# Branch products one pair later, w_out's splits over twelve stages, and one more step behind each softmax, in a hybrid decoder layer

## The chip, the cores and the metric

The kernel runs on one NeuronCore of a Trainium2 chip. The metric is device time in microseconds (us), from the start to the end of one execution. Five engines work beside each other, each through its own queue in order: TensorE (PE; its weight loads are listed apart as PEld), VectorE (DVE), ScalarE (ACT), GpSimd (POOL) and SyncE (SP), which only starts DMA transfers here. An instruction waits at the head of its queue until what it needs is there, and everything behind it waits too.

## The reference, cut to what matters

One layer of a decoder, for a prompt of 1024 tokens and for 64 sample tokens (8 × 8). `D` is 1024, `W` is 512.

```python
h = rmsnorm(x, g_pre)
proj = h @ w_in                         # 7 slices of W columns, then 3 merge gates of D columns
p_in, p_gate, c_val, c_glu, c_gate, q, x_gate = [proj[..., i * W:(i + 1) * W] for i in range(7)]
merge_logits = proj[..., 7 * W:].reshape(B, S, 3, D)
a = pool_mix(...) * silu(p_gate)                                      # branch 0
u = c_val * sigmoid(c_glu)
bconv = silu(layernorm(causal_dwconv(u, width 31))) * silu(c_gate)    # branch 1
p = softmax(qh @ mk / sqrt(128))                                      # 4 heads, 256 memory tokens
cattn = (p @ mv) * silu(x_gate)                                       # branch 2
br = einsum('bsnw,nwd->bsnd', stack([a, bconv, cattn]), w_branch)
merged = sum_n sigmoid(merge_logits)[n] * br[n]
y = merged @ w_out
x_new = x + rmsnorm(y, g_post)
```

## The kernel before

**Products.** Everything is held transposed: channels on the 128 partitions, the 1088 tokens along the row. Matrices are float32; each operand is split into a float16 part and the float16 rest (`hilo`: L75 on ACT for the first, L77 or, with a scale, L79 on DVE for the rest), and a product is three matmuls per piece of the inner dimension (`mm3`, L85, L88, L89). The projections and the output product use a Strassen-like scheme: `pair` (for a pair of 128-column blocks of w_in) makes seven products of twelve matmuls of 512 columns over seven sums of weights and the seven sums of h, which lie split in `BO` under the names `B11`, `T1`, `T2`, `B21`, `T3`, `T4`, `B22`. The sums of weights are made by accumulating DMAs on POOL's queue (L499 to L507), a `post` (L466) on DVE finishes an output block, and the 64 sample tokens get small products of 64 columns. `sig_pair` is a pair for gates, with the sigmoid (L664) on ACT.

**Branches and merge.** `merge(bi, ...)` multiplies branch `bi` with its part of w_branch and with its gates and sums over the branches, for four pairs of output tiles (`dp`). Call the gates of a pair G0 to G3 (seven stages each) and its branch products B0 to B3 (six stages each: two tiles by three groups of 364, 364 and 360 tokens, `TOK`; the third holds the samples). A branch product is twelve matmuls of 364 columns into a bank `pb`; L1151 on DVE multiplies the bank with the gate tile. The gated tile becomes `M[d]` in the first merge; in later ones an accumulating DMA (L1157) on POOL's queue adds it, and for the last pair of the last merge a DVE add (L1153). Stages run G0 B0 G1 B1 G2 B2 G3 B3. The merges come as 2 (attention), 0 (pooling), 1 (convolution).

**What sets the order.** The kernel writes a list `stages`. The main loop emits, at stage s: the loads of stage s + 12, the weight sums of s + 8, the weight splits of s + 3, the matmuls of s, a number of convolution taps (`conv_step`: L714, one DVE instruction of 1024 columns per tap, 31 taps for each of four channel tiles), the evictions of s, what hangs behind s, and some steps of the *jobs*. Taps and job steps per stage are the section's rates. A job is a generator (the heads' attention `head`, the samples' attention, the pooling groups, the convolution's samples); each `yield` ends a step. `until("prompt", bi)` behind a stage runs jobs until that branch's prompt part is there. A scheduler then places the emitted instructions on the engines' queues.

**Attention.** `head` does scores, `softmax_rows` (maximum L823, exponential L826, reciprocal L828, scaling L830), and in the next step the transposes (L851 on PE) and the product with the values. `sample_attention` does the same for the samples (transposes L935); at its end L951 multiplies the attention's output with its gate and L75/L77 split it into X[2], the operand of merge(2)'s third token group. `conv_samples` and the start of the convolution (L712, L725, L728, L729) share DVE and POOL with it.

**Buffers.** `Q` is a ring of 20 large buffers (gate tiles, M, X, keys, taps, w_out's first four row blocks), `raw` one of 4 for weights, `ws` one of 13 for split weights; PSUM has 4 banks `pm` and 4 banks `pb`.

**The tail.** Behind merge(1) comes `out_pair`, the product with w_out. It uses the places in `BO`, which become free as the last gates end: `wo_split` splits pieces of w_out into a freed place (L75, L79), `wo_less` subtracts blocks of w_out on POOL (L1208). A table hangs them on the stages from `last_pair`, the first stage of G3 in merge(1). `samples_split` (L77, 128x64) splits the samples' part of M.

## Time and profile before

| | |
|---|---|
| times of three runs | 934.6, 937.97, 1017.92 us (median 937.97) |
| profiled execution | 935.87 us, span 933.8 us |
| mean granted TensorE clock | 0.970 |
| instructions | 15219 |
| HBM read, written | 62.37 MB, 6.33 MB |

The span is what the profile's records cover, the execution's own time is 2.1 us longer. Times of the stages are counted from the span's start. In the profile, `pm L85 <- ...` names the tile written, the line of the instruction, and behind the arrow what was waited for; numbers behind tile names are left out.

```profile
## 2 busy tenths in 40 slices
PE   5869999899999869999989989999999999968996
...
DVE  4698599999968999999999696559565544699876
...
PEclk8889999999999988999999999999999999998998
```

Each digit is the busy share, in tenths, of one of 40 equal slices of 23.3 us; the last row is the granted clock of TensorE. Slices 1 to 3 are the start-up, the tenth to fourteenth the heads' and samples' attention, the fifteenth to twenty-first merge(2) and the pooling projections beside the taps, the last four the end of merge(1) and the output product.

### The profile page before, as it was taken

To read this page: it belongs to the slowest core of one execution; us is meant where nothing else is said; L and a number is where in the kernel's file an instruction comes from. 1 tells how busy PE (TensorE), PEld (TensorE's weight loads), DVE (VectorE), ACT (ScalarE), POOL (GpSimd) and SP (SyncE) were. 2 spreads that over 40 slices of the span, in tenths; PEclk is the share of its full clock that TensorE was granted. 3 is DMA by queue.
4 is the path that set the end of the run, shared out by engine and by line. 5 is a ranking of instruction groups with operands and counts; after the bars stand their busy time and mean duration, and the time that the engine had idled before them with its cause. 6 is when DMAs were issued, how large, how long until landed. Compare 5 with 4: busy or idle time off the path is not lost.

```text
span 933.8 us, 15219 instructions
## 1 busy us (share of the span) xinstructions
PE 858.4 (92%) x5765; PEld 459.7 (49%) x5765; DVE 741.3 (79%) x1141; ACT 452.8 (48%) x964; POOL 359.3 (38%) x384
## 2 busy tenths in 40 slices
PE   5869999899999869999989989999999999968996
PEld 3325444554455435555444545555545555535532
DVE  4698599999968999999999696559565544699876
ACT  7767446564653613323345444346445443545542
POOL 1364152344243380311235664516364213285500
PEclk8889999999999988999999999999999999998998
DMA  8635742225556222334444345545554656310132
GB/s 296 160 62 157 205 107 57 58 68 136 126 191 159 91 39 79 70 79 93 97 97 102 73 102 116 121 97 105 123 122 101 138 131 216 85 57 24 69 124 90
DMA packets 99238, 103.23 MB, mean 111 GB/s; under 512 B 5231, under 2 KB 71781, under 8 KB 99149
## 3 DMA queue, kind: packets, MB, share of 16 engines
q1 hardware_dynamic: 82748, 68.24, 23.3%
q0 software_dynamic: 16416, 34.02, 20.4%
q8 instruction: 45, 0.74, 0.3%
q14 instruction: 29, 0.23, 0.1%
HBM read 62.37 MB, written 6.33 MB: 74 GB/s over the span
## 4 chain that ended last, share of the span: by engine, by line
PE 40%; DVE 20%; issue 3%; DMA 2%; ACT 1%; POOL 0%; DVEq 0%; ACTq 0%; POOLq 0%
PE pm L85 10%; PE pm L88 9%; PE pm L89 9%; DVE q L714 6%; PE pb L88 4%; PE pb L89 3%; PE pb L85 3%; DVE ws L79 3%; DVE ws L77 2%; DMA raw<-raw 2%; DVE BO L79 1%; DVE q L1151 1%; DVE q L466 1%; DVE q L1090 1%; DVE q L1082 1%
## 5 line engine op out<-in xcount | busy, mean ns | idle before, releaser
L85 PE MATMUL pm<-BO,ws 128*128 128x512 f16 x836 | 320.7, 385 | 18.6 <-DVE q L787 4.8
L88 PE MATMUL pm<-BO,ws 128*128 128x512 f16 x836 | 321.2, 384 | 2.2 <-DVE BO L79 1.6
L89 PE MATMUL pm<-BO,ws 128*128 128x512 f16 x836 | 320.3, 384 | 1.2 <-DVE ws L77 0.9
L79 DVE SCALAR_TENSOR_TENSOR ws<-raw,ws 128x512 f16<-128x512 f32 x228 | 194.2, 869 | 60.1 <-ACT ws L75 58.5
L88 PEld LDWEIGHTS <-ws 128*128 128x128 f16 x1548 | 149.1, 99 | 135.4 <-issue 29.9
L85 PEld LDWEIGHTS <-ws 128*128 128x128 f16 x1548 | 148.8, 99 | 126.1 <-issue 17.2
L89 PEld LDWEIGHTS <-ws 128*128 128x128 f16 x1548 | 149.2, 99 | 123.5 <-issue 8.2
L75 ACT ACTIVATE ws<-raw 128x512 f16<-128x512 f32 x228 | 138.1, 625 | 121.8 <-PE pm L89 50.4
L714 DVE SCALAR_TENSOR_TENSOR q<-q,cw,q 128x1024 f32<-128x1024 f32 x120 | 174.2, 1462 | 0.2
L85 PE MATMUL pb<-q,ws 128*128 128x364 f16 (+1 forms) x288 | 92.2, 323 | 13.2 <-ACT q L75 8.4
L88 PE MATMUL pb<-q,ws 128*128 128x364 f16 (+1 forms) x288 | 92.5, 321 | 0.0
L89 PE MATMUL pb<-q,ws 128*128 128x364 f16 (+1 forms) x288 | 92.3, 321 | 0.0
L499 POOL DMA_DIRECT2D raw<-raw x25 | 21.9, 876 | 157.6 <-ACT raw L498 133.3
L513 ACT ACTIVATE h<-pm 128x512 f32<-128x512 f32 x75 | 44.2, 590 | 63.5 <-PE pm L89 63.3
L1151 DVE SCALAR_TENSOR_TENSOR q<-pb,q 128x364 f32<-128x364 f32 (+1 forms) x72 | 37.2, 527 | 22.1 <-PE pb L89 20.4
L466 DVE SCALAR_TENSOR_TENSOR q<-pm,h 128x512 f32<-128x512 f32 x51 | 34.8, 683 | 23.1 <-PE pm L89 13.2
L75 ACT ACTIVATE q<-q 128x1024 f16<-128x1024 f32 (+2 forms) x37 | 35.7, 972 | 29.6 <-DVE q L863 15.5
L507 POOL DMA_DIRECT2D raw<-raw x25 | 23.4, 935 | 66.3 <-issue 16.8
L506 POOL DMA_DIRECT2D raw<-raw x25 | 21.7, 867 | 65.6 <-DMA raw<-raw 25.3
L77 POOL TENSOR_TENSOR q<-q,q 128x1024 f16<-128x1024 f32 (+1 forms) x17 | 32.5, 1921 | 30.2 <-ACT q L75 30.2
L498 ACT ACTIVATE raw<-raw 128x512 f32<-128x512 f32 x50 | 30.9, 625 | 26.4 <-DVE ws L79 26.2
L85 PE MATMUL pm<-BS,ws 128*128 128x64 f16 x416 | 43.7, 194 | 0.0
(242 smaller groups left out, 1311.9 us busy)
## 6 DMA issues: line engine op xcount, KB each, us to landing
raw<-in_w_in SPq DMA_DIRECT2D x104, 256.0 KB, 3.0
raw<-raw POOLq DMA_DIRECT2D x100, 256.0 KB, 3.2
q<-in_x_prompt SPq DMA_DIRECT2D x16, 512.0 KB, 9.4
q<-q POOLq DMA_DIRECT2D x14, 544.0 KB, 5.8
raw<-in_w_branch SPq DMA_DIRECT2D x24, 256.0 KB, 3.8
q<-in_w_mem_kv SPq DMA_DIRECT2D x8, 512.0 KB, 6.8
q<-in_cache_mem_k SPq DMA_DIRECT2D x8, 512.0 KB, 3.7
q<-in_cache_mem_v SPq DMA_DIRECT2D x8, 512.0 KB, 9.4
```

What stands on the lines that cost most here:

```text
L75: nc.scalar.activation(hi, src, AF.Copy, scale=scale)
L77: (eng or nc.vector).tensor_tensor(lo, src, hi, ALU.subtract)
L79: nc.vector.scalar_tensor_tensor(lo, src, scale, hi, ALU.mult, ALU.subtract)
L85: ins = nc.tensor.matmul(out, wh, xh, start=start and j == 0, stop=False, skip_group_check=partial)
L88: nc.tensor.matmul(out, wh, xl, start=False, stop=False, skip_group_check=partial)
L89: nc.tensor.matmul(out, wl, xh, start=False, stop=stop and j == n - 1, skip_group_check=partial)
L466: nc.vector.scalar_tensor_tensor(dst, ps, sc, base, ALU.mult, ALU.add)
L498: nc.scalar.activation(A(1, kh), A(1, kh), AF.Copy, scale=-1.0)
L507: nc.gpsimd.dma_start(out=A(0, 1), in_=A(0, 0), accum_op=ALU.add)
L513: nc.scalar.activation(v[name], ps, AF.Copy, scale=sc)
L714: ins = nc.vector.scalar_tensor_tensor(acc, src, wj, acc, ALU.mult, ALU.add)
L1151: nc.vector.scalar_tensor_tensor(g, p, 1.0 / WS, g, ALU.mult, ALU.mult)
```

## The change

In `merge` the gates of the next pair are emitted ahead of the branch products of a pair: G0 G1 B0 G2 B1 G3 B2 B3. What hung behind G0 (`until("prompt", bi)`) now hangs behind G1. `last_pair` moves with G3, from 13 to 19 stages before the end of the sections, and the table of w_out's splits goes from 10 to 14 stages behind it. In `head` and in `sample_attention` one more `yield` stands between the softmax and the transposes. Lines behind the edits move by 1, 2 or 11: L935 becomes L937, L951 L953, L1007 L1009, L1151 L1162, L1153 L1164, L1157 L1168, L1208 L1219.

```diff
--- before.py
+++ after.py
@@ -844,6 +844,7 @@
                     mm3(p[:, a, :], [(q[:, 0, tk : tk + P], q[:, 1, tk : tk + P], kT[:, 0, h, :], kT[:, 1, h, :])])
                 softmax_rows(p, 2, prs[:, tp * 2 : tp * 2 + 2, :])
             yield
+            yield
             pT = Q([P, 2, 2, HALF], F16)
             for c in range(2):
                 p = pb()
@@ -929,6 +930,7 @@
             vr = kr
             pr = half((P, 1, NMEM))
             softmax_rows(sc[:, :NMEM].rearrange("p (a m) -> p a m", a=1), 1, pr)
+            yield
             yield
             p = pb()
             for c in range(2):
@@ -1117,9 +1119,18 @@
     M = [None] * KT
 
     def merge(bi, first, last):
+
+        sgs = []
+
+        def gates(dp):
+            if dp < KT // 2:
+                sgs.append({})
+                sig_pair(GATE0 + bi * D + dp * 2 * P, sgs[dp])
+
+        gates(0)
         for dp in range(KT // 2):
-            sg = {}
-            sig_pair(GATE0 + bi * D + dp * 2 * P, sg)
+            gates(dp + 1)
+            sg = sgs[dp]
             if dp == 0:
                 after(until("prompt", bi))
             v = {}
@@ -1187,7 +1198,7 @@
         section()
 
 
-    last_pair = len(stages) - 13
+    last_pair = len(stages) - 19
     WO = [None] * KT
     gp = {}
 
@@ -1212,12 +1223,12 @@
     for s, f in [
         (0, lambda: (wo_split(B11, 0, 0), wo_less(0, 1, (0, 1), (0, 0)))),
         (2, lambda: wo_split(T1, 0, 1)),
-        (5, lambda: wo_split(B21, 1, 0)),
-        (6, lambda: (wo_split(B22, 1, 1), wo_less(1, 1, (1, 1), (0, 1)))),
-        (7, lambda: wo_split(T2, 1, 1)),
-        (8, lambda: wo_less(0, 0, (1, 1), (0, 0))),
-        (9, lambda: (wo_split(T3, 0, 0), wo_less(1, 0, (1, 0), (1, 1)))),
-        (10, lambda: wo_split(T4, 1, 0)),
+        (6, lambda: wo_split(B21, 1, 0)),
+        (8, lambda: (wo_split(B22, 1, 1), wo_less(1, 1, (1, 1), (0, 1)))),
+        (10, lambda: wo_split(T2, 1, 1)),
+        (11, lambda: wo_less(0, 0, (1, 1), (0, 0))),
+        (12, lambda: (wo_split(T3, 0, 0), wo_less(1, 0, (1, 0), (1, 1)))),
+        (14, lambda: wo_split(T4, 1, 0)),
     ]:
         stages[last_pair + s][4].append(f)
```

How this moves instructions is seen at three places. The first is TensorE's queue at the samples' softmax, first before the change: `h_3253` and `h_3360` are the softmax's result, `pb_3074` and `pb_3154` its scores, `pm` banks belong to gates, `pb` banks with 364 columns to branch products.

```order
L88 MATMUL pb_3074<-q_3205,q_1311 32x256
L89 LDWEIGHTS q_1311
L89 MATMUL pb_3074<-q_3205,q_1311 32x256
L935 MATMUL pb_3261<-ident,h_3253 128x128 x2
L85 LDWEIGHTS ws_3272
L85 MATMUL pb_3516<-q_1633,ws_3272 128x364
L88 LDWEIGHTS ws_3272
L88 MATMUL pb_3516<-q_1633,ws_3272 128x364
```

Behind the change the same place of the queue reads (`...` stands for gate matmuls):

```order
L88 LDWEIGHTS q_1311
L88 MATMUL pb_3154<-q_3333,q_1311 32x256
L89 LDWEIGHTS q_1311
L89 MATMUL pb_3154<-q_3333,q_1311 32x256
L85 LDWEIGHTS ws_3368
L85 MATMUL pm_3387<-BO,ws_3368 128x512
...
L89 LDWEIGHTS ws_3823
L89 MATMUL pm_3888<-BO,ws_3823 128x512
L937 MATMUL pb_3404<-ident,h_3360 128x128 x2
L742 MATMUL pb_3620<-ident,q_2722 30x128
L743 MATMUL pb_3620<-ident,v_3621 64x128
```

Before, the transposes (L935) follow the last score product. After, 27 gate matmuls stand between: twelve into `pm_3387`, twelve into `pm_3862` and three into `pm_3888`; the rows left out are these.

The second is VectorE's queue around L787 of `q_4902`, the last gate step of the pooling branch before which TensorE is held, first before the change. L714 are convolution taps, L794 the samples' piece of the same gates, L1007 (L1009) a pooling group's product, L79 splits of weights.

```order
L466 SCALAR_TENSOR_TENSOR h_4900<-pm_4824,h_4898 128x512
L79 SCALAR_TENSOR_TENSOR ws_5061<-raw_4631,ws_5061 128x512
L77 TENSOR_TENSOR q_4785<-q_4779,q_4785 128x1024
L794 SCALAR_TENSOR_TENSOR q_4883<-pm_4908,q_4883 128x64
L714 SCALAR_TENSOR_TENSOR q_3952<-q_2856,cw,q_3952 128x1024
L787 SCALAR_TENSOR_TENSOR q_4902<-pm_4800,q_4902 128x512
L79 SCALAR_TENSOR_TENSOR ws_5115<-raw_4634,ws_5115 128x512
L794 SCALAR_TENSOR_TENSOR q_4902<-pm_4908,q_4902 128x64
L466 SCALAR_TENSOR_TENSOR h_4999<-pm_4824,h_4863 128x512
L714 SCALAR_TENSOR_TENSOR q_3952<-q_2856,cw,q_3952 128x1024
L1007 SCALAR_TENSOR_TENSOR q_4883<-pb_5004,psc,q_4883 128x364
L79 SCALAR_TENSOR_TENSOR ws_5151<-raw_4848,ws_5151 128x512
```

Behind the change, around the same L787, the queue reads:

```order
L714 SCALAR_TENSOR_TENSOR q_3962<-q_2799,cw,q_3962 128x1024
L79 SCALAR_TENSOR_TENSOR ws_4978<-raw_4848,ws_4978 128x512
L79 SCALAR_TENSOR_TENSOR ws_4984<-raw_4631,ws_4984 128x512
L79 SCALAR_TENSOR_TENSOR ws_5025<-raw_4845,ws_5025 128x512
L794 SCALAR_TENSOR_TENSOR q_4883<-pm_4908,q_4883 128x64
L79 SCALAR_TENSOR_TENSOR ws_5028<-raw_4848,ws_5028 128x512
L466 SCALAR_TENSOR_TENSOR h_4900<-pm_4824,h_4898 128x512
L79 SCALAR_TENSOR_TENSOR ws_5061<-raw_4631,ws_5061 128x512
L794 SCALAR_TENSOR_TENSOR q_4902<-pm_4908,q_4902 128x64
L1009 SCALAR_TENSOR_TENSOR q_4883<-pb_5004,psc,q_4883 128x364
L787 SCALAR_TENSOR_TENSOR q_4902<-pm_4800,q_4902 128x512
L79 SCALAR_TENSOR_TENSOR ws_5115<-raw_4634,ws_5115 128x512
```

Before, taps alternate with the splits up to and past L787; after, the last tap (`q_3962`) stands ten rows ahead of it, and one L794 and one L1009 more stand ahead of it. In the whole queue ahead of L787 there are 117 taps before and 120 after; ahead of the earlier L466 of `q_4667` (529 rows in), 103 and 109.

The third is VectorE's queue at the split of w_out into `B22`, first before the change. `BO<-raw` and `BO<-q` are rests of w_out, `ws_8600` the samples' part of M, L1151 (L1162) branch products.

```order
L79 SCALAR_TENSOR_TENSOR BO<-raw_8128,BO 128x512
L79 SCALAR_TENSOR_TENSOR BO<-raw_8158,BO 128x512
L466 SCALAR_TENSOR_TENSOR q_8200<-pm_8145,h_8172 128x512
L79 SCALAR_TENSOR_TENSOR BO<-raw_8174,BO 128x512
L79 SCALAR_TENSOR_TENSOR BO<-raw_8203,BO 128x512
L77 TENSOR_TENSOR ws_8600<-q_3238,ws_8600 128x64
L77 TENSOR_TENSOR ws_8600<-q_3291,ws_8600 128x64
L77 TENSOR_TENSOR ws_8600<-q_3733,ws_8600 128x64
L77 TENSOR_TENSOR ws_8600<-q_3755,ws_8600 128x64
L77 TENSOR_TENSOR ws_8600<-q_4055,ws_8600 128x64
L77 TENSOR_TENSOR ws_8600<-q_4077,ws_8600 128x64
L1151 SCALAR_TENSOR_TENSOR q_8200<-pb_8349,q_8200 128x364
```

Behind the change the rows at the split of `B22` are:

```order
L1162 SCALAR_TENSOR_TENSOR q_7793<-pb_8222,q_7793 128x364
L79 SCALAR_TENSOR_TENSOR BO<-raw_8033,BO 128x512
L79 SCALAR_TENSOR_TENSOR BO<-raw_8066,BO 128x512
L466 SCALAR_TENSOR_TENSOR q_8108<-pm_8053,h_8080 128x512
L79 SCALAR_TENSOR_TENSOR BO<-raw_8082,BO 128x512
L1162 SCALAR_TENSOR_TENSOR q_7793<-pb_8236,q_7793 128x364
L79 SCALAR_TENSOR_TENSOR BO<-raw_8111,BO 128x512
L79 SCALAR_TENSOR_TENSOR BO<-raw_8033,BO 128x512
L1162 SCALAR_TENSOR_TENSOR q_7793<-pb_8262,q_7793 128x360
L79 SCALAR_TENSOR_TENSOR BO<-raw_8066,BO 128x512
L79 SCALAR_TENSOR_TENSOR BO<-q_7975,BO 128x512
L1162 SCALAR_TENSOR_TENSOR q_7813<-pb_8280,q_7813 128x364
```

Before, the samples' splits stand behind the splits of `B22` and ahead of the last branch evictions; after, the evictions of B2 and B3 alternate with the splits of w_out, and the eight samples' splits come twelve to twenty-two rows behind the last of them.

## Prediction

> **What bounds the kernel now.** I read the page first, then busy time by stage, then TensorE's waits, then the rows around each wait. The two page lines are busy us, share of the span and instruction count per engine, and the costliest VectorE group.
>
> ```profile
> PE 858.4 (92%) x5765; PEld 459.7 (49%) x5765; DVE 741.3 (79%) x1141; ACT 452.8 (48%) x964; POOL 359.3 (38%) x384
> L714 DVE SCALAR_TENSOR_TENSOR q<-q,cw,q 128x1024 f32<-128x1024 f32 x120 | 174.2, 1462 | 0.2
> ```
>
> TensorE at 92% is the bound on average, but an average says nothing of a stage. The next rows are windows: from:to in us, length, then busy time and count of PE, PEld, DVE, ACT and POOL, the granted clock, DMA share, GB/s.
>
> ```profile
> 98.00:334.00 236.00, 223.04 (x1611) 123.79 (x1610) 204.15 (x288) 125.71 (x262) 90.65 (x78) 0.99 0.44 115
> 316.00:322.00 6.00, 4.13 (x18) 2.42 (x19) 5.93 (x9) 3.75 (x6) 1.48 (x1) 0.72 0.29 103
> 334.00:502.00 168.00, 152.87 (x1027) 80.64 (x1026) 168.00 (x192) 60.04 (x120) 49.70 (x45) 0.96 0.37 80
> 345.00:355.00 10.00, 5.92 (x30) 2.77 (x30) 10.00 (x13) 2.73 (x8) 3.36 (x2) 0.50 0.11 20
> 450.00:460.00 10.00, 8.09 (x64) 3.96 (x62) 10.00 (x12) 3.42 (x8) 4.41 (x6) 0.83 0.30 54
> 486.00:496.00 10.00, 7.35 (x37) 3.36 (x35) 10.00 (x9) 3.43 (x7) 6.16 (x5) 1.00 0.49 128
> 560.00:820.00 260.00, 258.92 (x1740) 141.33 (x1739) 153.09 (x248) 122.62 (x245) 100.60 (x99) 1.00 0.53 122
> 829.00:854.00 25.00, 19.22 (x131) 9.90 (x131) 24.45 (x45) 10.22 (x32) 17.83 (x26) 0.80 0.24 74
> ```
>
> From 560 to 820 PE is busy 258.92 of 260 at full clock, so whatever moves inside those 260 us can't bring anything. From 334 to 502 VectorE is busy 168.00 of 168: there it is the bound, and PE waits for its queue. In 98 to 334 VectorE idles 236 − 204.15 = 31.85 us. So three places can give time: the attention stretch before 334, the VectorE stretch, and the tail from 820. Their waits, as waiter, what released it, total us, times, longest:
>
> ```profile
> PE pb L935 <- DVE h L830: 4.0, 1, 4.0
> PE pb L851 <- DVE q L830: 3.7, 5, 1.6
> PE pb L85 <- ACT q L75: 8.5, 2, 8.4
> PE pm L85 <- DVE q L466: 3.9, 3, 1.9
> PE pm L85 <- DVE q L787: 2.7, 1, 2.7
> PE pb L85 <- DVE q L1151: 4.8, 1, 4.8
> PE pm L85 <- ACT ws L75: 2.3, 1, 2.3
> PE pb L88 <- DVE ws L77: 2.0, 2, 1.1
> PE pm L89 <- DVE ws L77: 0.9, 1, 0.9
> ```
>
> The first two are the transposes behind a softmax (samples, heads). The third is the first branch products of the samples in merge(2). The fourth and fifth lie in 440 to 560. The last four are the tail, 10.0 us together.
>
> A lowered clock costs beside the wait: lost time is (1 − clock) × window, so 0.28 × 6 = 1.7 us at the samples' transposes, 0.50 × 10 = 5.0 us at merge(2), 0.20 × 25 = 5.0 us in the tail. The waits that the change aims at (4.0 + 3.7 + 8.4 + 10.0 = 26.1) and this clock loss (11.7) make 37.8 us. That is the most that can go, and the question is how much of it is given back.
>
> **The change part by part.** No arithmetic is added or removed: in each of three merges, three of the four groups of six branch products move behind the gates of the next pair. The sum is made against the profiled execution, 935.87 us (span 933.8 and 2.1 around it); the median of the three times is 937.97, so 0.2% higher.
>
> *The extra step at the heads (L851) and samples (L935).* The next rows are start, us, engine, line and operation, with idle time and its releaser in brackets.
>
> ```profile
> 313.92 0.42 DVE L823 TENSOR_REDUCE t<-pb 128x1 f32<-128x256 f32 x1 [0.77 <-PE pb L89]
> 317.38 0.35 DVE L830 TENSOR_SCALAR h<-h,t 128x256 f32<-128x256 f32 x1
> 317.87 0.66 PE L935 MATMUL pb<-ident,h 128*128 128x128 f32 x2 [3.99 <-DVE h L830]
> 791.76 0.54 DVE L1151 SCALAR_TENSOR_TENSOR q<-pb,q 128x364 f32<-128x364 f32 x1 [1.32 <-PE pb L89]
> 793.61 0.54 DVE L1151 SCALAR_TENSOR_TENSOR q<-pb,q 128x364 f32<-128x364 f32 x1 [1.31 <-PE pb L89]
> ```
>
> The samples' softmax takes from 313.9 to 317.7, and PE has nothing to do for 3.99 us of it. In the new order 27 gate matmuls of 512 columns stand between the last score product and the transposes. A branch product of 12 matmuls of 364 columns is evicted every 793.61 − 791.76 = 1.85 us where PE sets the pace: 154 ns each, so 217 ns at 512 columns, and 27 of them are 5.8 us. That covers 3.99 us and the clock loss. At the heads an extra step is one product more (2.6 us) against a longest wait of 1.6. I take all of 4.0 + 3.7 = 7.7 us as gone from PE here (the 1.7 of clock I keep for the range).
>
> *What VectorE makes of it.* The next rows are one line's own view (minimum, median and maximum of an instruction, in ns) two groups in the window 440 to 540, and VectorE's two largest waits in 98 to 334.
>
> ```profile
> L714 DVE SCALAR_TENSOR_TENSOR q<-q,cw,q x61: 1264/1269/3077, 359.5 to 498.7; 128x1024 f32<-128x1024 f32 x61
> L1007 DVE SCALAR_TENSOR_TENSOR q<-pb,psc,q 128x364 f32<-128x364 f32 x6 | 3.4, 588 | 0.7 <-POOL q L789 0.7
> L794 DVE SCALAR_TENSOR_TENSOR q<-pm,q 128x64 f32<-128x64 f32 x4 | 0.9, 214 | 0.0
> DVE ws L79 <- ACT ws L75: 13.5, 8, 7.8
> DVE q L77 <- ACT q L75: 9.6, 6, 3.4
> ```
>
> From 334 its queue is full, so PE arriving 7.7 us earlier is worth only what VectorE, too, gets ahead. It has 31.85 us of idle time before 334, much of it spent waiting for the same products, so it can follow. But the new order puts other work ahead of the places where PE is held last. Ahead of the row L787 of q_4902, which frees PE at 489.5, stand 117 conv taps (L714) before and 120 after, with one more evicted tile (L1007) and one more 64-column piece (L794): 3 × 1.27 + 0.6 + 0.2 = 4.6 us. That gives 4.6 − 7.7 = **−3.1 us**. Bounds: −4.8 if the clock loss goes too; +7.6 (6 × 1.27) if VectorE doesn't get ahead and what counts is the earlier hold at L466 of q_4667, ahead of which 109 taps stand where 103 stood.
>
> *The 8.4 us in merge(2).* Its cause is a queue on VectorE:
>
> ```profile
> 335.76 4.34 DVE L712 TENSOR_SCALAR q<-q,cw,parT 128x1024 f32<-128x1024 f32 x1
> 343.41 5.00 DVE L729 TENSOR_SCALAR q<-v,parT 128x32 f32<-128x32 f32 x1
> 348.33 0.41 DVE L951 TENSOR_TENSOR sxs<-pb,sxs 128x256 f32<-128x256 f32 x1
> ```
>
> The samples' attention output is written by L951 only at 348.33, behind the conv starts L712 and L729. Between the last product of that attention and the first branch tile with samples PE now has three branch products (3 × 1.85) and 26 gate matmuls (5.6), 11.2 us. Before it ran dry after 5.2 and waited 8.4, so 13.6 are needed, and 2.4 of the wait should be left at this place. But VectorE is full here, and PE is held again by L787 140 us later. What PE gains at 349 it waits for there, so I count it at **0**. Bounds: −13.4, wait and clock, if VectorE isn't what holds L787; 0.
>
> *Q buffers.* A third set of gate tiles is alive: 8 of M, 4 of X, 4 of w_out and 6 of gates are 22 for 20 places where merges end, so a pair's first sigmoid waits for the accumulating DMA of the pair before last.
>
> ```profile
> q<-q POOLq DMA_DIRECT2D x14, 544.0 KB, 5.8
> ```
>
> It lands 5.8 us after issue (median). Four gate products of 2.6 us lie before the first sigmoid needs it: 10.4 against 5.8, hidden; cost 0, and up to 6 if the cover is gone. The accumulating DMAs (L1157) of a moved group move behind the next pair's weight sums on GpSimd's queue, and its w_branch loads behind that pair's w_in loads on SyncE's; both have a pair's time (seven products, 18 us) until someone needs them, against 3 to 6 us of transfer, 0 as well.
>
> *The tail.* Six branch products, 6 × 1.85 = 11.1 us of PE work, now come behind the last gates, so that the slot B22 of the split w_out is free 11.1 us earlier and the splits have longer stages.
>
> ```profile
> 817.16 1.29 DVE L79 SCALAR_TENSOR_TENSOR BO<-raw,BO 128x512 f16<-128x512 f32 x2 [0.22 <-ACT BO L75]
> 818.98 2.84 DVE L79 SCALAR_TENSOR_TENSOR BO<-raw,BO 128x512 f16<-128x512 f32 x2
> 821.74 7.40 DVE L77 TENSOR_TENSOR ws<-q,ws 128x64 f16<-128x64 f32 x6
> 848.87 4.58 DVE L77 TENSOR_TENSOR ws<-sr,ws 128x128 f16<-128x128 f32 x12
> 854.05 0.69 DVE L602 SCALAR_TENSOR_TENSOR h<-pm,h 128x512 f32<-128x512 f32 x1 [0.60 <-PE pm L89]
> 817.93 3.34 POOL L1208 TENSOR_TENSOR raw<-raw,q 128x512 f32<-128x512 f32 x2 [8.75 <-DVE BO L79]
> ```
>
> From the B22 split (817.16) to the first output eviction (854.05) VectorE runs through 55 instructions; after, 78 stand there. The extra ones are 6 evictions like those at 793.61 (0.54 each, 3.2), one add of that size (0.54) and 16 pieces of L77 at 4.58 / 12 = 0.38 (6.1): 9.8 us. So −11.1 + 9.8 = −1.3 if VectorE is as hindered as before. It is hindered: while GpSimd's subtractions L1208 run, two L79 take 2.84 where two took 1.29, and six tiny L77 take 7.40, 1.23 each against 0.38 for pieces twice as wide. Without that hindrance these two rows would be 2.84 − 1.29 + 7.40 − 6 × 0.38 = 6.7 us shorter, and the sum −8.0. The six tiny pieces now stand behind the evictions that PE waits for, but the number of subtractions stays: I take the middle, **−4.7**, with 1 us of the clock's 5.0. Bounds: −15.0 (wait and clock, all of it), and 3.7 + 16 × 1.23 − 11.1 = +12 if GpSimd hinders all the 16 extra pieces as it did the tiny ones.
>
> The clock part can be weighed otherwise. The Trainium skill, page "TensorE: Matmul & The Clock Gate", section "What's actually happening", has the clock halved after an idle window of about 3.4 us. The 2.7 us wait in 486:496 left it at 1.00, which agrees; the 1.9 us wait in 450:460 shows 0.83, which doesn't. By the page remaining waits of 2 us would leave the clock full, and the sum would come to 4 us less; I go by the trace.
>
> Sum: −3.1 + 0 + 0 − 4.7 − 1.0 = −8.8, so 935.87 − 8.8 = **927**. Forecast: most of the stalls that the change removes come back as PE waiting for a full VectorE, and a small gain stays.
>
> **The rivals.** *A: all the targeted stalls go.* VectorE gets far enough ahead in 98 to 334 to take the 8.4 along, and the tail is covered: 935.87 − 37.8 = 898. For it: 31.85 us of idle time, and a tail where each wait is short. Against it: 168.00 of 168, and taps that don't become fewer.
>
> *B: slower.* The taps ahead of L466 and L787 decide. If VectorE's idle time before 334 doesn't shrink (23.1 of it is waiting for ScalarE's halves of splits, L75, not for PE's products directly), the six extra taps push L466 by 7.6 us and nothing comes back: 943, with a tail that gains nothing. The point is about 6 us of the 31.85: below it B, above it the forecast. The Trainium skill, page "SBUF — State Buffer", section "Who interferes with whom", lets a VectorE instruction with two SBUF inputs contend with a GpSimd one that reads SBUF, which the L77 row at 7.40 fits; splits spread over more stages would then meet the same subtractions for longer, on B's side.
>
> *C: nothing is left.* PE reaches L787 and the last splits when it did; both stretches are VectorE's: 933 to 940.
>
> **How the numbers follow.** Forecast 917 to 933: 0.55. A, below 917: 0.20. C, 933 to 940: 0.15. B, above 940: 0.10. The range leaves out the better half of A and the worse half of B, and stops short of the tail's +12 alone, 948: 906 to 943. A difference of 2%, 18.7 us, is about what a measurement of this kernel tells from no change: faster is below 917.2, slower above 954.6. Faster 0.22 (A and a little of the forecast), slower 0.04 (B with buffers that collide), same 0.74.
>
> **What would show it.** L851 and L935 without waits of over 1 us, and 316:322 at full clock; PE's wait for L75 in merge(2) under 5 us; VectorE still without idle time for 150 us and more, and PE's waits for L466 and L787 grown from 6.6 to over 10 us; from 560 to 820 no change in pace; tail waits of about 5 us. I am wrong if VectorE's full stretch is much shorter (then A), or if waits appear on Q buffers at the sigmoids (L664) or on the accumulating DMAs.

## The result and the profile after

The changed kernel takes 939.5 us (median of 20 runs), the kernel before 934.16 (20 runs): a ratio of **1.0065**, 95% interval 1.0050 to 1.0079. The ratio is made from the fast runs alone (one of the kernel before was slow, 1017.92 us) and is not the quotient of the two medians. By the bound of 2% that is no change; by the interval it is a small loss where a gain of 1% was forecast. The profiled execution took 938.34 us (before 935.87).

The page's first line of engines and the costliest VectorE group, after:

```profile
PE 861.6 (92%) x5765; PEld 460.5 (49%) x5765; DVE 733.9 (78%) x1141; ACT 454.7 (49%) x964; POOL 363.1 (39%) x384
L714 DVE SCALAR_TENSOR_TENSOR q<-q,cw,q 128x1024 f32<-128x1024 f32 x120 | 173.6, 1451 | 0.4
```

Nothing is seen there. The windows (columns as in the prediction) say more:

```profile
98.00:334.00 236.00, 220.95 (x1565) 121.03 (x1564) 210.27 (x292) 128.04 (x267) 96.18 (x82) 0.99 0.47 121
316.00:340.00 24.00, 14.50 (x102) 7.42 (x101) 23.69 (x18) 12.40 (x20) 17.09 (x6) 0.82 0.30 100
334.00:502.00 168.00, 153.14 (x1055) 81.89 (x1054) 152.69 (x183) 56.63 (x112) 47.51 (x40) 0.96 0.31 71
340.00:364.00 24.00, 23.88 (x203) 13.43 (x202) 23.93 (x29) 6.86 (x16) 4.71 (x2) 0.90 0.09 27
560.00:820.00 260.00, 258.58 (x1733) 140.94 (x1731) 155.17 (x234) 122.54 (x228) 101.86 (x93) 1.00 0.50 115
```

VectorE idles 236 − 210.27 = 25.7 us before 334 (31.85 before the change), and it is no longer full from 334 to 502: 152.69 of 168. Yet PE is no earlier. PE's largest waits over the whole run (`...` marks rows left out, most of them of the start-up):

```profile
PE pm L85 <- ACT h L513: 12.3, 7, 7.0
PE pb L85 <- DVE q L1162: 9.4, 4, 4.7
PE pb L85 <- ACT q L75: 6.9, 2, 4.3
PE pb L88 <- DVE ws L77: 5.4, 1, 5.4
...
PE pb L937 <- DVE h L830: 2.9, 2, 2.0
PE pm L85 <- DVE q L466: 2.6, 2, 2.4
...
PE pb L852 <- DVE q L830: 1.3, 1, 1.3
PE pm L85 <- DVE q L787: 1.3, 1, 1.3
```

The heads' waits are nearly gone (3.7 to 1.3), the 8.4 us in merge(2) are gone, and a new one of 7.0 us for L513 stands at the top. Where the time went is seen when both traces are set to PE's own work (the sum of the issue distances of its matmuls), since the order changed. The table gives how much later (+) or earlier (−) PE comes to that point than in the kernel before, with the difference at 80 us of work, the start-up, taken out; single executions differ by about 3 us.

| PE's own work done, us | what lies there | changed | heads' step alone | merge(1) and table alone | step on both sides |
|---|---|---|---|---|---|
| 250 | end of the heads | −3.0 | −7.2 | −0.1 | −5.1 |
| 260 | the kernel before has its wait at the samples' softmax behind it | −7.7 | −11.5 | −0.1 | −10.0 |
| 280 | the changed kernel has its waits there behind it | +5.8 | +8.8 | +0.9 | +1.7 |
| 300 | merge(2), the wait of 8.4 us before is past | −3.7 | −0.8 | −0.7 | −9.8 |
| 340 | merge(2) | +0.2 | +0.1 | −1.0 | −6.5 |
| 480 | pooling projections, behind the last taps | +5.5 | +3.4 | −0.9 | −3.8 |
| 720 | start of the tail | +6.3 | +2.9 | −2.0 | −2.9 |
| 820 | end | +4.0 | 0.0 | −3.5 | −4.2 |

The changed kernel is 3.0 us ahead at the end of the heads, and 7.7 when the kernel before has stood at its samples' softmax (wait L935). It loses 13.5 when it stands there itself, wins back 9.5 where the old wait in merge(2) stood, and loses 9.2 up to the pooling projections behind the last taps. The samples' softmax in the changed kernel, in the timeline of PE:

```profile
326.52 0.59 PE L85 MATMUL pm<-BO,ws 128*128 128x512 f16 x1 [6.97 <-ACT h L513]
337.19 0.41 PE L937 MATMUL pb<-ident,h 128*128 128x128 f32 x2 [2.03 <-DVE h L830]
```

The same in ScalarE's timeline (`...` is a row left out):

```profile
324.00 1.28 ACT L826 ACT_TABLE_LOAD   x1
325.42 0.47 ACT L826 ACTIVATE h<-pb,t 128x256 f32<-128x256 f32 x1
...
325.89 0.59 ACT L513 ACTIVATE h<-pm 128x512 f32<-128x512 f32 x1
```

And in VectorE's, with rows left out:

```profile
322.45 2.61 DVE L79 SCALAR_TENSOR_TENSOR ws<-raw,ws 128x512 f16<-128x512 f32 x1
324.98 0.41 DVE L823 TENSOR_REDUCE t<-pb 128x1 f32<-128x256 f32 x1
325.31 2.81 DVE L714 SCALAR_TENSOR_TENSOR q<-q,cw,q 128x1024 f32<-128x1024 f32 x1
330.64 3.06 DVE L714 SCALAR_TENSOR_TENSOR q<-q,cw,q 128x1024 f32<-128x1024 f32 x1
336.70 0.34 DVE L830 TENSOR_SCALAR h<-h,t 128x256 f32<-128x256 f32 x1
```

The gate product that should cover the softmax needs the copy L513 of an earlier product of its bank. On ScalarE that copy stands right behind the exponential L826, which waits for the maximum L823 on VectorE. So PE stands still from 319.55, when the scores are done, to 326.52, in spite of 27 matmuls to do. Both queues come to the exponential together: L823 ends at 325.39, and the table load ahead of the exponential on ScalarE, behind copies of V, at 325.28. VectorE then needs 12 us from L823 to L830 (3.8 before), with taps at 2.8 and 3.1 us in between.

### The profile page after: what moved, and what is told of

It reads as the page before. It is cut to its first block, busy times and chain, and to the rows that moved or that the text cites. A ratio compares the mean times of both kernels' runs of the same rounds, so it can differ in the third digit from the quotient of the medians.

```text
span 936.5 us, 15198 instructions
## 1 busy us (share of the span) xinstructions
PE 861.6 (92%) x5765; PEld 460.5 (49%) x5765; DVE 733.9 (78%) x1141; ACT 454.7 (49%) x964; POOL 363.1 (39%) x384
## 5 line engine op out<-in xcount | busy, mean ns | idle before, releaser
L79 DVE SCALAR_TENSOR_TENSOR ws<-raw,ws 128x512 f16<-128x512 f32 x228 | 191.6, 855 | 57.7 <-ACT ws L75 56.2
L75 ACT ACTIVATE ws<-raw 128x512 f16<-128x512 f32 x228 | 137.5, 626 | 113.1 <-PE pm L89 43.3
L714 DVE SCALAR_TENSOR_TENSOR q<-q,cw,q 128x1024 f32<-128x1024 f32 x120 | 173.6, 1451 | 0.4
L85 PE MATMUL pb<-q,ws 128*128 128x364 f16 (+1 forms) x288 | 93.8, 326 | 9.4 <-DVE q L1162 9.4
L89 PE MATMUL pb<-q,ws 128*128 128x364 f16 (+1 forms) x288 | 94.0, 326 | 0.0
L88 PE MATMUL pb<-q,ws 128*128 128x364 f16 (+1 forms) x288 | 93.8, 326 | 0.0
L499 POOL DMA_DIRECT2D raw<-raw x25 | 21.8, 873 | 152.4 <-ACT raw L498 152.1
L513 ACT ACTIVATE h<-pm 128x512 f32<-128x512 f32 x75 | 44.3, 590 | 48.9 <-PE pm L89 47.8
L466 DVE SCALAR_TENSOR_TENSOR q<-pm,h 128x512 f32<-128x512 f32 x51 | 34.8, 684 | 26.1 <-PE pm L89 12.9
L1162 DVE SCALAR_TENSOR_TENSOR q<-pb,q 128x364 f32<-128x364 f32 (+1 forms) x72 | 37.7, 527 | 19.9 <-PE pb L89 19.9
L506 POOL DMA_DIRECT2D raw<-raw x25 | 22.1, 884 | 71.5 <-DVE ws L79 32.0
L507 POOL DMA_DIRECT2D raw<-raw x25 | 21.9, 877 | 69.1 <-DVE ws L79 18.5
L75 ACT ACTIVATE q<-q 128x1024 f16<-128x1024 f32 (+2 forms) x37 | 35.6, 971 | 24.7 <-DVE q L864 7.9
L664 ACT ACTIVATE q<-q 128x512 f32<-128x512 f32 x36 | 22.6, 628 | 44.3 <-DVE q L466 43.9
L505 POOL DMA_DIRECT2D raw<-raw x25 | 21.9, 878 | 53.8 <-DMA raw<-raw 53.1
```

Source lines behind the costliest of these rows:

```text
L75: nc.scalar.activation(hi, src, AF.Copy, scale=scale)
L79: nc.vector.scalar_tensor_tensor(lo, src, scale, hi, ALU.mult, ALU.subtract)
L85: ins = nc.tensor.matmul(out, wh, xh, start=start and j == 0, stop=False, skip_group_check=partial)
L88: nc.tensor.matmul(out, wh, xl, start=False, stop=False, skip_group_check=partial)
L89: nc.tensor.matmul(out, wl, xh, start=False, stop=stop and j == n - 1, skip_group_check=partial)
L466: nc.vector.scalar_tensor_tensor(dst, ps, sc, base, ALU.mult, ALU.add)
```

## Experiments

All ratios are against the kernel before on the same chip, with 95% intervals. "Queue theory" and "step theory" are the names under which the recorded expectations speak of the places of the steps; "tap theory" and "VectorE theory" of VectorE's load.

**The parts alone.** The edits: the extra `yield` in both generators, in one, or in none, and for the gates a choice of the merges that have them ahead:

```diff
-        gates(0)
+        if bi in AHEAD: gates(0)
         for dp in range(KT // 2):
-            gates(dp + 1)
+            gates(dp + (bi in AHEAD))
```

Where merge(1) isn't in `AHEAD`, `last_pair` and the table of splits are the old ones.

Both steps, no gates ahead.

> Before plus the two extra steps behind the softmax, nothing else. Queue theory (in the changed kernel the gate products that should cover the samples' softmax wait for a copy L513 that stands behind the exponential on ScalarE; it takes both the extra step and the gates moved ahead): no such wait here, the heads' 3.7 us and the samples' 4.0 us go, PE is 4 to 8 us ahead at 310 us, and half of it or more is kept: ratio 0.992 to 0.997. Tap theory (VectorE is the bound from 334 to 502 and holds PE whatever comes before): the gain at 310 us is there but gone at 510 us, ratio 0.999 to 1.001.

Measured 939.36 us, **1.0057** (1.0033 to 1.0081): outside of both. PE is 5.3 us ahead at the end of the heads (250 us of its work), and then waits longer than before at both places (PE's waits over the run):

```profile
PE pb L85 <- ACT q L75: 15.5, 2, 14.5
...
PE pb L937 <- DVE h L830: 7.4, 1, 7.4
```

Gates ahead in merge(2) alone.

> Before plus gates ahead in merge(2) alone, without the extra steps, the other merges and the tail as before. Queue theory: the wait for L513 behind the exponential (7.0 us in the changed kernel) doesn't form without the extra step, the 8.4 us wait of merge(2) shrinks to some 2 us, and the kernel is at 0.990 to 0.998. Tap theory: six more conv taps stand ahead of the gates' evictions whatever the steps are, PE loses 4 to 8 us between 360 and 510 us: 1.004 to 1.009.

Measured 937.0, **1.0035** (1.0014 to 1.0055). That lies between the two ranges, nearer to the tap theory's. The wait of 8.4 us is gone and comes back as L466, 6.1 us from 300 to 360 and 4.5 from 360 to 440, with VectorE at 168.00 of 168 in 334 to 502: given back. But not by the taps that the expectation named: ahead of L466 of `q_4667` there are 103 of them, as before; the 109 come from the steps.

Merge(1) and the table alone.

> Before plus gates ahead in merge(1) alone with the new table of w_out's splits; merges 2 and 0 and the attention as before. If the loss is made before 510 us, as the two traces suggest (PE 0.9 us further back over the tail's start, 2.9 us regained at its end), this alone gives 0.996 to 0.999. If the tail is what makes the change slower (splits under GpSimd's subtractions, 12 us in the prediction's bound), 1.004 or more.

Measured 933.09, **0.9998** (0.9984 to 1.0012): nothing won, nothing lost.

All gates ahead, no steps.

> The changed kernel without its two extra steps: all merges with gates ahead, the new table. Queue theory: as the sum of merge(2) alone and the tail alone, 0.988 to 0.998, so faster than the changed kernel by 0.9% or more. Tap theory: the heads' 3.7 us come back on top of the loss, 1.006 to 1.012.

Measured 937.12, **1.0036** (1.0022 to 1.0051), in neither range, and the same as merge(2) alone: merge(0) and the tail add nothing that shows, and the steps are not what makes merge(2) lose.

The heads' step alone.

> Before plus the extra step in the heads alone. With both steps PE was 9.1 us ahead after 260 us of its work (where the heads end) and 15 us behind 20 us of work later, at the samples' softmax. Step theory: the heads' step is the gain and the samples' step the loss, so here PE is 7 to 9 us ahead at the end of the heads and the samples' part is as before; some of the lead is lost to a full VectorE: 0.993 to 0.998. Rival (VectorE takes all of it back by 510 us): 0.999 to 1.002. Rival (the loss at the samples comes from the heads' earlier end, which puts more conv taps ahead of the samples' softmax on VectorE): 1.003 or more, with a long wait at L935 or in merge(2) as with both steps.

Measured 936.42, **1.0026** (1.0007 to 1.0045). The lead (7.2 us at 250 us of PE's work) is lost at once at the samples' softmax. Its transposes wait 11.4 us (4.0 before), since L830 comes at 327.43 (317.38 before). PE's wait:

```profile
PE pb L936 <- DVE h L830: 11.4, 1, 11.4
```

VectorE's timeline:

```profile
327.43 0.34 DVE L830 TENSOR_SCALAR h<-h,t 128x256 f32<-128x256 f32 x1
```

Ahead of it on VectorE stand 54 taps where 49 stood, and eleven more instructions in all. The step in the heads is taken eight times, so the samples' softmax is emitted some stages later, and each stage emits its taps and weight splits first. That was the second rival's mechanism; the ratio is just below its bound.

The samples' step alone.

> Before plus the extra step in the samples' attention alone. Step theory: everything behind the samples' softmax comes a step later, the wait in merge(2) grows from 8.4 to some 14 us and the wait at L935 (with this step's line number) from 4.0 to some 7 us: 1.006 to 1.014. Rival (the heads' earlier end is to blame): 0.998 to 1.002, waits as before.

Measured 940.58, **1.0078** (1.0050 to 1.0107): the expected size, but not at the expected waits (L466 11.8 us in all, nothing at L935). The changed kernel without it.

> The changed kernel without the extra step in the samples' attention; the heads' step, all gates ahead and the new table stay. Step theory: the wait of 7.0 us for L513 behind the exponential goes, the heads' lead stays: 0.994 to 1.000 against before, so at least 0.6% faster than the changed kernel. Rival (gates ahead in merge(2) is what loses, the steps only add): 1.003 to 1.007.

Measured 944.7, **1.0115** (1.0084 to 1.0147), the opposite of the step theory: the parts don't add, and beside the heads' step and the gates the samples' step helps. Here the transposes wait 16.6 us for L830. Ahead of L823, for which ScalarE waits 7.45 us, stands one split that took 9.11 us, until four instructions of GpSimd in a row (L77, L725, L77, L725, 318.18 to 326.80) had ended:

```profile
318.25 9.11 DVE L79 SCALAR_TENSOR_TENSOR ws<-raw,ws 128x512 f16<-128x512 f32 x1
```

So a part of this result may be which instructions of the two engines happen to meet; no run isolates it. Heads' step with the tail.

> Before plus the heads' extra step and gates ahead in merge(1) with the new table: the parts that have shown a gain or nothing. The tail alone gave 0.9998. Step theory: 0.992 to 0.998, the fastest so far. Rival (VectorE takes the heads' lead back): 0.999 to 1.001.

Measured 937.54, **1.0049** (1.0029 to 1.0070): a miss, no better than the heads' step alone.

**Taps and steps per stage.** The rates (taps, job steps) of three sections are changed, in the changed kernel and in the one before:

```diff
-RATES = [(1.1, 2.2), (1, 1.4), (0.9, 1), (1, 1.2), ...
+RATES = [(1.1, 2.2), (0.8, 1.4), (0.7, 1), (0.8, 1.2), ...   # fewer taps
+RATES = [(1.1, 2.2), (1, 1.8), (0.9, 1.3), (1, 1.5), ...     # more steps
```

> The changed kernel with fewer conv taps per stage in the sections before merge(2) (rates 0.8, 0.7, 0.8 for 1, 0.9, 1). Ahead of L830 of the samples' second softmax on VectorE stand 49 taps as before the change; in the changed kernel 59, and PE passes L937 after 275 us of its own work in both. Softmax-queue theory (the extra steps move the samples' softmax behind more conv taps on VectorE, and what PE does in the meantime waits for that softmax too): the waits at L937 and for L513 behind the exponential fall from 9.0 us to under 3, and PE is 5 to 10 us ahead of before at 300 us of work; ratio 0.990 to 0.999. ScalarE theory (the exponential and the copies of V on ScalarE hold L513 whatever VectorE does): that wait stays at 5 us or more, ratio 1.004 to 1.008.

Measured 936.3, **1.0033** (1.0015 to 1.0052): half of the loss, and between the two ranges. So is the wait at L513, and L830 comes at 329.5 although only 49 taps stand ahead of it. L823 ends at 318.07 here, but the exponential starts at 318.88, when the table load ahead of it on ScalarE ends (318.86): what is left of the wait comes from ScalarE's own queue.

```profile
PE pm L85 <- ACT h L513: 4.0, 1, 4.0
```

> The kernel before with the same lower rates of taps, as a control. 40 taps stand ahead of the samples' L830 where 49 stood. Softmax-queue theory: its softmax was released 4 us behind its products already, so little is to be had there, the wait in merge(2) may shrink, and the taps come back later: 0.996 to 1.004. Rival (fewer taps ahead are a gain in any kernel): 0.985 to 0.995, and the same gain as between the changed kernel and its version with fewer taps.

Measured 962.81, **1.0315** (1.0285 to 1.0345). The taps that are left out early come in a bunch ahead of later evictions (14 in a row, 24.7 us, from 407.20), and PE waits for those:

```profile
PE pm L85 <- DVE q L466: 23.2, 3, 19.4
```

This is the mechanism of the prediction's rival B at full size: what stands ahead of an eviction on VectorE is PE's time.

> The changed kernel with more job steps per stage in the same sections (1.8, 1.3, 1.5 for 1.4, 1, 1.2), so that the added steps no longer delay the samples: their transposes stand behind 259.7 us of PE work as before the change (274.7 in the changed kernel), their L830 behind 42 taps (59). Softmax-queue theory: waits at L937 and L513 together under 4 us, merge(2) without a wait over 4 us, ratio 0.990 to 0.999. Rival (the gates ahead in merge(2) lose by themselves, as the kernel with that part alone did): 1.002 to 1.005.

Measured 936.2, **1.0024** (1.0003 to 1.0046): the waits at the samples are gone, 8.4 us for L466 take their place. The ratio is the rival's.

> The kernel before with the same higher rates of job steps, as a control. The samples' transposes come after 251.9 us of PE work, their L830 behind 38 taps. The wait of 8.4 us in merge(2) should shrink by half or more. If VectorE's full stretch takes it back, 0.998 to 1.002; if not, 0.990 to 0.996, and then the steps' rate is worth more than the change.

Measured 933.13, **1.0003** (0.9983 to 1.0024): PE is 7.5 us ahead after 290 us of work and level again at 340. VectorE takes it back, as the expectation's first branch said.

**VectorE relieved.** Every tap but a channel's first works on half of its columns:

```diff
-nc.vector.scalar_tensor_tensor(acc, src, wj, acc, ALU.mult, ALU.add)
+nc.vector.scalar_tensor_tensor(acc[:, :HALF], src[:, :HALF], wj, acc[:, :HALF], ALU.mult, ALU.add)
```

> The kernel before, with every conv tap but the first of a channel on half of its columns (the other half of the convolution is left out): some 0.5 us less for each of 116 taps on VectorE. If VectorE's full stretch from 334 to 502 us is what sets the time there, its waits go for the most part: 0.975 to 0.988. If not, 0.993 to 1.000.

> The changed kernel, the same half of the convolution left out. VectorE theory (the change saves PE's waits at the softmaxes, and a full VectorE takes this back and more, since more of its work stands ahead of the samples' softmax): with VectorE relieved the change gains, so this is 4 to 15 us faster than the kernel before with half taps. Place theory (the longer way to the samples' softmax, in ScalarE's and PE's queues, costs whatever VectorE's load is): 2 to 7 us slower than it, as with whole taps.

Measured 926.34, **0.9928** (0.9904 to 0.9953), and 924.97, **0.9911** (0.9889 to 0.9933). The window of 334 to 502 in the kernel before with half taps:

```profile
334.00:502.00 168.00, 155.36 (x1015) 81.13 (x1014) 130.08 (x199) 64.64 (x126) 45.71 (x50) 0.97 0.38 84
```

And in the changed kernel with half taps:

```profile
334.00:502.00 168.00, 158.93 (x1091) 84.75 (x1090) 124.84 (x192) 61.80 (x120) 46.35 (x49) 0.97 0.35 80
```

VectorE now has some 40 us of idle time there, and the kernel before is only 7 us faster, less than expected: VectorE's load was not the whole bound. The change is no loss any more (1.4 us between the medians, and the intervals overlap), so neither theory's number came. And the wait for L513 at the samples is still there, 7.7 us at the longest. It isn't made by taps: ScalarE waits 4.30 us for L823, and ahead of that stands one L79 that took 7.19 us (from 313.97) beside GpSimd.

```profile
PE pm L85 <- ACT h L513: 14.8, 6, 7.7
```

**GpSimd's rests of V.** The samples' attention splits V with the rest on GpSimd; this leaves that rest out, and puts the first half in its place:

```diff
-hilo(vr, vb[:, 0], vb[:, 1], eng=nc.gpsimd)
+nc.scalar.activation(vb[:, 0], vr, AF.Copy)      # and vb[:, 0] for vb[:, 1] in the products
```

> The changed kernel without GpSimd's rests of V in the samples' attention (the first half of V stands in for its rest in the products, so PE's work stays and this part of the result is coarser). In the changed kernel GpSimd makes three of them, 2.9 us each, during the samples' second softmax, and VectorE's instructions there take 2.6 to 3.1 us where 0.7 to 1.3 is usual. If this hindrance is a part of the loss: L830 ends 6 to 9 us earlier than at 337, waits at L937 and L513 together fall from 9.0 to 4 or less, 1.000 to 1.004. If VectorE's full stretch takes it back: 1.005 to 1.008.

> The kernel before without GpSimd's rests of V in the samples' attention, as the control. Its softmax was not hindered (3.8 us from L823 to L830), so the wait at L935 stays at 4 us; L712 and L729 may come faster and the wait in merge(2) shrink: 0.996 to 1.001.

Measured 931.34, **0.9976** (0.9957 to 0.9995), and 926.87, **0.9931** (0.9906 to 0.9956). L830 of the changed kernel comes at 326.7 in place of 336.7, and the kernel gains 0.9%, more than expected, though its wait for L513 is still 6.4 us where 4 or less was expected (the exponential, at 321.04, again follows ScalarE's own table load and not L823, which ends at 320.27). The one before gains 0.7%, outside of its range too, and its wait at L935 grew to 7.5. So the hindrance costs both kernels, and the change still loses 0.5% without it (931.34 against 926.87): it isn't the change's loss, or only a small part of it. The same rests on VectorE (`hilo(vr, vb[:, 0], vb[:, 1])`) in the kernel before.

> The kernel before with the rests of V in the samples' attention on VectorE in place of GpSimd: eight instructions of 128x1024, 1.2 to 1.5 us each, so some 10 us more for VectorE, and none of GpSimd's that hinder it. Leaving these rests out gave 0.9931. If the hindrance was the price and VectorE has room for them before 334 us (31 us idle there), 0.993 to 0.998, faster than both kernels. If VectorE's queue is what counts, 1.000 to 1.006.

Measured 934.88, **1.0017** (0.9996 to 1.0039): no gain, in the range of the second branch. That VectorE's queue takes it is not shown apart.

**ScalarE's order.** A further step ahead of the softmax puts, among much else, the copy L513 ahead of the exponential:

```diff
             pr = half((P, 1, NMEM))
+            yield
             softmax_rows(sc[:, :NMEM].rearrange("p (a m) -> p a m", a=1), 1, pr)
             yield
             yield
```

> The changed kernel with one more step in the samples' attention, ahead of the softmax. On ScalarE the copy L513 on which the next gate products wait now stands 19 rows ahead of the exponential of the samples' second softmax; in the changed kernel it stands right behind it. On VectorE nearly nothing changes ahead of L830 (60 taps, 59 in the changed kernel), on TensorE 24 gate matmuls (5.2 us) stand between scores and transposes, and can start. ScalarE theory (the order there is what defeats the cover): no wait for L513 of over 2 us at the samples, the wait at L937 stays under 5 us, 2 to 5 us faster than the changed kernel, 1.001 to 1.004. VectorE theory (its queue ahead of the softmax sets L830, whatever the cover): the wait only moves to L937, 6 us or more there, 1.005 to 1.008.

Measured 932.62, **0.9987** (0.9966 to 1.0008), so 0.8% faster than the changed kernel, with one line. PE's timeline at the samples' softmax:

```profile
321.72 0.38 PE L85 MATMUL pm<-BO,ws 128*128 128x512 f16 x1 [2.73 <-DVE q L466]
334.52 0.66 PE L938 MATMUL pb<-ident,h 128*128 128x128 f32 x2 [7.47 <-DVE h L830]
```

The windows of 316 to 340 and 340 to 364 of the same kernel:

```profile
316.00:340.00 24.00, 13.81 (x102) 7.69 (x99) 24.00 (x20) 8.85 (x15) 14.46 (x6) 0.86 0.22 70
340.00:364.00 24.00, 24.00 (x223) 14.00 (x221) 23.66 (x32) 10.51 (x21) 7.88 (x5) 1.00 0.20 38
```

The wait for L513 is gone, as the ScalarE theory said; but 10.2 us of waits stand here against 9.0, at L938 as the VectorE theory said. What is saved in these 48 us is the clock: (0.18 + 0.10) × 24 = 6.7 us lost in the changed kernel, 0.14 × 24 = 3.4 here. The other half of the gain lies before the softmax and between 380 and 400 us of PE's work, and no run isolates it. No version is faster than the kernel before beyond its interval, apart from those that leave work out.

## Why the prediction was wrong, step by step

- **Heads: right in size.** The wait L851 went from 3.7 to 1.3, and PE was 3.0 us ahead at the end of the heads where the sum has 3.7.
- **The cover of the samples' softmax: failed.** "27 of them are 5.8 us. That covers 3.99 us and the clock loss." They stood, 6.97 us, for L513 behind L826. The step counted the covering matmuls and not what their own bank waits for on ScalarE. In place of −4.0 stand 9.0 us of waits. The clock loss wasn't covered either: from 316 to 364 us it is 6.7 us, as in the kernel before (0.93 and 0.79 in the two windows).
- **"VectorE, too, gets ahead": failed.** Its idle time before 334 did shrink, by 6.1 us, just past the prediction's own point between forecast and rival B, so by that point the forecast should have come. But the lead went into taps, as that line's own view in the changed kernel shows, and then VectorE's timeline:

```profile
L714 DVE SCALAR_TENSOR_TENSOR q<-q,cw,q x73: 1269/1274/3917, 301.7 to 478.8; 128x1024 f32<-128x1024 f32 x73
```

```profile
489.03 0.69 DVE L787 SCALAR_TENSOR_TENSOR q<-pm,q 128x512 f32<-128x512 f32 x1 [3.59 <-ACT q L664]
```

  The last tap starts at 478.8, 20 us earlier than before (498.7), and L787 of `q_4902` runs at 489.03, where it ran at 488.75; now it waits for ScalarE, on an idle VectorE, and ScalarE waited 3.54 us for the product itself, so it is PE that comes late. The term of −3.1 was 0 there, and PE is 5.5 us behind at 480 us of its work. Between 362 and 500 us PE waits 11.4 us, 6.2 before: L513 1.5 and L466 2.4 (377 and 384 us), L1162 at a branch bank 3.2 (426, with a clock of 0.94 in 412:440), L75 at the pooling groups' operands 4.3 (477). What puts each of them there is open. Nor was VectorE's full stretch the bound that the prediction took it for: with 38 us of its work there taken out, the kernel before is only 7 us faster.
- **The 8.4 us in merge(2) at 0: right in the sum.** The wait went and was given back: in the changed kernel at the samples' softmax ahead of it, in merge(2) alone at L466 behind it.
- **The taps: right count, wrong source.** 109 against 103 come with the steps, and L466 behind them runs at 453.58, where it ran at 453.17. They are a price, as fewer of them in the changed kernel returned half of the loss, but beside the places of the steps, not alone.
- **Q buffers and the middle: right.** No wait on a Q buffer; 258.58 of 260 busy.
- **The tail: failed, −5.7 measured as 0** (0.9998 alone). The interval of that run is −1.5 to +1.1 us. In the table PE gains 1.5 us there, and 2.3 in the changed kernel, from 720 us of work to the end, within what single executions differ by. The hindrance did not halve, it met another instruction, one L79 instead of six small L77. VectorE's timeline, changed:

```profile
825.87 6.31 DVE L79 SCALAR_TENSOR_TENSOR BO<-raw,BO 128x512 f16<-128x512 f32 x1
832.10 0.53 DVE L1162 SCALAR_TENSOR_TENSOR q<-pb,q 128x364 f32<-128x364 f32 x1
```

And GpSimd's (L1168 starts a DMA):

```profile
825.51 1.56 POOL L1219 TENSOR_TENSOR q<-raw,q 128x512 f32<-128x512 f32 x1
826.74 1.54 POOL L1219 TENSOR_TENSOR raw<-raw 128x512 f32<-128x512 f32 x1
827.94 1.17 POOL L1168 DMA_DIRECT2D q<-q  x1
828.56 1.85 POOL L1219 TENSOR_TENSOR q<-raw,q 128x512 f32<-128x512 f32 x1
829.79 1.83 POOL L1219 TENSOR_TENSOR raw<-raw 128x512 f32<-128x512 f32 x1
```

  The L79 ends 0.56 us behind the fourth subtraction (the next one, at 832.55, takes 0.68), and the eviction behind it holds PE for 4.7 us. With merge(1) alone the same L79 takes 6.32 and PE waits 4.7. The Trainium skill, page "SBUF — State Buffer", section "Who interferes with whom", has such a pair exclude one another for a whole instruction; the L79 has two inputs in SBUF and fits that, but it was held over four of GpSimd's subtractions, not over one. The tail's waits are 11.4 us, 10.0 before: evictions 5.3 (4.8), the samples' splits L77, which now come last, 5.4 + 0.7 (2.9), splits L75 0 (2.3).
- **The rivals.** The time lies in C's range (933 to 940), but not by C's mechanism: VectorE was not full (152.69 of 168), and PE was ahead, behind and ahead again before it came late. That the number is C's is chance. B's mechanism is a part of it. A did not come near, though the prediction's sign for A, a shorter full stretch of VectorE, did; PE's waits for L466 and L787, expected to grow from 6.6 to over 10 us, fell to 3.9. The sign of the forecast rested on −3.1 and −5.7, and neither was there.

Shown are the places (parts alone, table), the price of order on VectorE (fewer taps in the kernel before), that a relieved VectorE or one more step ahead of the samples' softmax each removes the loss, and that GpSimd's hindrance costs both kernels alike, but for 0.2%. Not shown is that the further step helps by ScalarE's order: as much is waited for at that place as without it. Nor is it shown how VectorE's and ScalarE's queues share the loss; at the exponential they arrive together.

## What to carry to other kernels

Work that is to cover a wait must itself be free to run: follow the bank and the operands of the covering instruction into every other engine's queue, and look what stands ahead of them there. Where an order is made of stages that emit a share of each kind of work, one more step moves everything behind it past all that the stages emit, so count the rows ahead of the awaited instruction, not only the step. Idle time that shrinks on a second engine is a lead only if that engine does what is waited for with it.

## What the runs showed of the hardware

GpSimd's instructions at the samples' softmax of the changed kernel, rests of V (L77) and then products of the samples' convolution (L725):

```profile
321.48 8.62 POOL L77 TENSOR_TENSOR q<-q,q 128x1024 f16<-128x1024 f32 x3 [1.30 <-ACT q L75]
330.06 5.63 POOL L725 TENSOR_TENSOR q<-us,cw 128x992 f32<-128x992 f32 x2
```

VectorE's taps took 2.8 to 3.1 us beside them where 1.27 is the median. Leaving the rests of V out was worth 0.7% in the kernel before, more than any part of the change won. Where GpSimd's instructions stand without a gap, VectorE is held over several of them: one L79, 0.68 us alone, took 6.31 us over four in the tail and 9.11 us over four in the kernel without the samples' step.

The clock fell to 0.90 in 340 to 364 of the changed kernel, with PE busy 23.88 of 24 us there. It was at 0.50 in 338 to 341, behind the wait of 2.03 us, and at 0.57 in 348 to 352, behind no wait but behind some 95 matmuls of 8 columns each (345.8 to 348.2). The Trainium skill, page "TensorE: Matmul & The Clock Gate", section "What's actually happening", asks for an idle window of about 3.4 us; this trace doesn't agree, and no run isolates what lowered it.
